# Diffusion backbone on one core: the last modulation vectors computed in the last recurrence head instead of in the first ConvGLU

## The chip, the cores and the metric

The kernel runs on one core of a Trainium2 chip. The metric is the device time of one execution in microseconds. The planner (the framework's scheduler) orders the instructions of every engine when the kernel is built, from their program order, their priorities and a timeline that it works out itself; the order of an engine's instructions is then fixed, and semaphores let each wait for its operands. A change of the program can therefore move instructions far from the lines it touches.

## What is computed

Two layers over 512 latent tokens and 256 context tokens of width 1024. Layer 0 mixes tokens by windowed attention, layer 1 by a gated linear recurrence in both directions with 8 heads; each layer ends with a ConvGLU. Every sub-layer is a norm, scaled and shifted by vectors made from the conditioning. Cut to what matters here:

```python
for layer in range(DEPTH):
    last = layer == DEPTH - 1
    mod = jax.nn.silu(c) @ ada_w[layer] + ada_b[layer]
    mod_c = jax.nn.silu(c_ctx) @ ada_w[layer] + ada_b[layer]
    sh1, sc1, g1, sh2, sc2, g2 = jnp.split(mod[:, None, :], 6, axis=-1)
    ...
    hx = rms_norm(x, norm1_g[layer]) * (1.0 + sc1) + sh1
    ...
        yx, yc = hgrn2_bidir(hx, hc, hgrn_w_in[j], hgrn_w_out[j], hgrn_o_gain[j], lb_sched[layer], not last)
    x = x + g1 * yx
    hx2 = rms_norm(x, norm2_g[layer]) * (1.0 + sc2) + sh2
    x = x + g2 * conv_glu(hx2, ffn_w_up[layer], ffn_conv_w[layer], ffn_conv_b[layer], ffn_w_down[layer])
```

The six vectors of a layer are computed in three ranges of 2048 columns of `ada_w`: range 0 holds sh1 and sc1, range 1 g1 and sh2, range 2 sc2 and g2. Layer 1's sc2 is first used where the recurrence's output is scaled for the second ConvGLU, its g2 in that ConvGLU's down product.

## The kernel before

**Products.** Each large product is done in three passes: weights and activations are split into a high part (a ScalarE copy, `wh`, L117 or L140) and a low part (a VectorE subtraction, `wl`, L118 or L141), and PE multiplies high by high, high by low, low by high (`mm_steps`, L170). A weight block comes by one or two DMAs on SP's queue into a raw buffer of 8 KB per partition (`load_raw`, L95, tile `wr`, two buffers in all), and is split into operand tiles of 512 columns, taken in turn from the pools in the list `self.wsp` (`operand`). In the recurrence that list holds three pools in turn: `ws0` with four buffers, `wsC` and `wsD` with two each. The splits are given a priority 180 instructions ahead of their place (`W_AHEAD`).

**Vectors.** `ada_steps` (L307 to L324) computes one range: eight loads of 1 MB of `ada_w` into the same two raw buffers (tile `wada`), after each of them four plain fp32 products of 32 output rows side by side in the array (`ada`, L309), then a VectorE copy to SBUF (`adas`, L314), four transposes (`adat`, L318), the addition of the bias (`mod`, L324) and, for range 2, the scale of the second norm (`gs`). It is a generator that yields after each step, so that another loop can lay its steps between its own. Ranges 0, 1 and 2 of layer 1 are drawn by the first ConvGLU: one step ahead of each of its 22 column tiles (`next(side)`), and one in each of its first five down rounds.

**The recurrence** (`hgrn`). For each head `front` makes the forget gates (`pf`) and the query (`pq`), `back` the value (`pv`, transposed as `pvT`, copied to `v`) and the gate (`pgate`), all from PE into PSUM tiles of two banks in the pool `pj`, two buffers. `scan` is the head's chain of dependent steps. It has seven levels: in each, ScalarE gathers the keys into `Y`, PE makes small products (`lv` at L1134 in levels 0 to 4, `at` at L1147 and L1149 in levels 5 and 6), and VectorE multiplies the queries (`Q`, L1158) and the keys (`K`, L1159) for the next level. Then the tail: transposes (`kT`), state products (`U`), the states (`S`, L1204 and L1206), the output (`po`), its norm (`osq`, `oss`, `or`, `oR`), and `oT`, which is split into `oh` (L1240, L1241). Its PSUM tiles are those of the pools `sc` and `lv`, one bank each, two buffers.

While a head's chain runs, the steps of the generator `fill` are traced between its own: `back` of this head and `front` of the next; for the last head, in place of the next `front`, `begin_out`. That starts the output product `ho`: its columns come in four pairs (`dp`), each in one tile of `pj`, and for pairs 0 and 1 the parts of heads 0 to 6 are done while the last head's chain still runs. When the last head's `oh` is there, `hgrn_out` adds its part to pairs 0 and 1 and does pairs 2 and 3; behind each pair VectorE adds to the stream (`xl`, L908), ScalarE scales it by `gs` (`y`, L375), and the operands of the second ConvGLU are made from that (`combos`, `hs`, L383, L384, L396).

**Pools of PSUM.** In the recurrence `pj` takes the first four of the eight banks, then `sc` two and `lv` two. Before and after it one pool takes all eight for a ConvGLU.

Of the kernel before, what the change touches and what calls it, by code (L numbers as in the profile page):

```python
# [8 lines left out]
F32 = mybir.dt.float32  # L9
# [5 lines left out]
PSUM = bass.MemoryType.PSUM  # L15

P = 128
D = 1024
KT = D // P
# [49 lines left out]
def f(t):  # L69
    return t.bitcast(F32)  # L70


class Kernel:
    def __init__(self, tc, a, dbg=None):
        self.tc, self.nc, self.a, self.dbg = tc, tc.nc, a, dbg or {}
# [958 lines left out]
    def hgrn(self, hn, R, acc, hb, pj, lv, sc):  # L1034
        nc, a = self.nc, self.a
        win = a["hgrn_w_in"][0]
        act = lambda k: (hn[:, 0, k], hn[:, 1, k])
        es = ExitStack()
        h1 = self.pool(es, "h1", 1)
# [6 lines left out]
        rows = self.row_factor(acc, False, h1, sc, "sc", 512, R, 1.0, (h1, "dg"))  # L1046
# [18 lines left out]
        def front(h, s):  # L1065

            wf = self.load_w([cw(1024 + h * P), cw(2048 + h * P)])
            wq, s["wv"] = self.load_w([cw(h * P), cw(3072 + h * P)])
            T = h1.tile([P, 2, TOK], F32, tag="T", name="T")
            K2 = h1.tile([P, 2, TOK], F32, tag="K2", name="K2")  # L1070
            for dr in range(2):
                ps = pj.tile([P, 1024], F32, tag="pj", name="pf")
                yield from steps(ps, wf[dr], NFULL)
                for _ in rows:
                    pass
                z = h1.tile([P, TW], F32, tag="sg", name="z", bufs=2)
                nc.vector.tensor_tensor(z, ps[:, 0:TW], R, op=ALU.mult)
                i = 1 - dr
                nc.scalar.activation(T[:, i, 0:LAT], z[:, 0:LAT], AF.Sigmoid, bias=z[:, SH:SH + 1])
                nc.scalar.activation(T[:, i, LAT:TOK], z[:, C0:TW], AF.Sigmoid, bias=z[:, SH + 1:SH + 2])  # L1080
                nc.gpsimd.tensor_scalar(T[:, i], T[:, i], self.lb[:, 1, h:h + 1], self.lb[:, 0, h:h + 1], op0=ALU.mult, op1=ALU.add)
                nc.gpsimd.tensor_scalar(K2[:, i], T[:, i], -1.0, 1.0, op0=ALU.mult, op1=ALU.add)
            yield from half(s, wq, "q")
            Q2 = h2.tile([P, 2, LAT], F32, tag="Q2", name="Q2")
            nc.vector.tensor_tensor(Q2, ap(s["q"][:, 0:1], 0, (0, 2), (1, LAT)), T[:, :, 0:LAT], op=ALU.mult)
            KK = h1.tile([P, LAT], F32, tag="KK", name="KK")
            nc.vector.tensor_tensor(KK, K2[:, 0, 0:LAT], K2[:, 1, 0:LAT], op=ALU.add)
            s.update(T=T, K2=K2, Q2=Q2, KK=KK)

        def back(h, s):  # L1090

            wg, = self.load_w([cw(4096 + h * P)])
            ps = pj.tile([P, 1024], F32, tag="pj", name="pv")
            yield from steps(ps, s["wv"], NFULL)
            z = h1.tile([P, TW], F32, tag="sg", name="zv", bufs=2)
            nc.vector.tensor_tensor(z, ps[:, 0:TW], R, op=ALU.mult)
            for lo, hi, c in ((0, LAT, SH), (C0, TW, SH + 1)):
                nc.scalar.activation(z[:, lo:hi], z[:, lo:hi], AF.Identity, bias=z[:, c:c + 1])
            yield from half(s, wg, "gate")
            pt = pj.tile([P, 1024], F32, tag="pj", name="pvT")  # L1100
            for i in range(6):
                t0 = i * P if i < NQ else C0 + (i - NQ) * P
                nc.tensor.transpose(pt[:, i * P:(i + 1) * P], z[:, t0:t0 + P], self.ident)
            v = h2.tile([P, 6, P], F32, tag="v", name="v")
            nc.scalar.activation(v, pt[:, :TOK].rearrange("p (t c) -> p t c", c=P), AF.Copy)
            s["v"] = v
# [128 lines left out]
        wout = a["hgrn_w_out"][0]  # L1235
        part = [None, [], []]

        def split_o(h):
            oh = part[0]
            nc.scalar.activation(oh[:, 0, h], oT[:, h], AF.Copy)  # L1240
            nc.vector.tensor_tensor(oh[:, 1, h], oT[:, h], f(oh[:, 0, h]), op=ALU.subtract)  # L1241

        def begin_out():

            part[0] = oh = hb.tile([P, 2, KT, LAT], F32R, tag="hn", name="oh1")
            for dp in range(2):
                w = self.load_w([self.wcols(wout, d * P, P) for d in (dp, dp + 4)])
                ps = pj.tile([P, 1024], F32, tag="pj", name="ho")
                part[1].append(w)
                part[2].append(ps)  # L1250
                for j in range(2):
                    out = [(ps[:, 512 * j:512 * j + 512], 0)]
                    for k in range(KT - 1):
                        if dp == 0 and j == 0:
                            split_o(k)
                        yield from self.mm_steps(w[j], (k,), lambda k: (oh[:, 0, k], oh[:, 1, k]), out, k == 0, False)

        ss = [{} for _ in range(KT + 1)]
        for _ in front(0, ss[0]):
            pass  # L1260
        for h in range(KT):
            def fill(h=h):
                yield from back(h, ss[h])
                yield from (front(h + 1, ss[h + 1]) if h + 1 < KT else begin_out())

            rest = fill()
            for n in scan(h, ss[h]):
                for _ in range(n):
                    next(rest, None)
            for _ in rest:  # L1270
                pass
# [36 lines left out]
    def run(self, stop=99):  # L1308
        nc, a = self.nc, self.a
        top = ExitStack()  # L1310
# [12 lines left out]

        xp = self.pool(top, "xp")
        self.xl = xp.tile([P, KT, LAT], F32, tag="xl", name="xl")
        self.wsp.append(self.pool(top, "wsC", 2))
        Rp = self.pool(top, "Rp", 1)
        pjs = ExitStack()
        pj = self.pool(pjs, "pj", 2, PSUM)
        hB = ExitStack()  # L1330
        hb = self.pool(hB, "hB")
        h1 = hb.tile([P, 4, 2, 4, 386], F32R, tag="hn", name="hs0")
# [3 lines left out]
        es = ExitStack()  # L1336
        tmp = self.pool(es, "tmpA", 1)
        acp = self.pool(es, "accA", 1)
        acc = Rp.tile([P, TOK], F32, tag="acc", name="acc0")
        hs = [*(h1[:, i] for i in range(4)), h2]  # L1340
# [8 lines left out]
        bk = self.pool(pjs, "bkA", 8, PSUM)  # L1349
        h3 = self.pool(rs, "hs2", right=True).tile([P, 2, 2, 4, 386], F32R, tag="hs", name="hs5")  # L1350
        hs += [h3[:, i] for i in range(2)]
        gp = self.pool(es, "gpA", 5)
        R = Rp.tile([P, 772], F32, tag="R", name="R0")
        rows = self.row_factor(acc, False, tmp, bk, "ps", 512, R, -1.0, (gp, "g"))
# [11 lines left out]
            self.scaled(1, 0, d, hn2[0], False)  # L1366

        self.ap_, self.ap_tag = Rp, "acc"
        self.ffn(0, hs, R, rows, False, tmp, acp, bk, gp, done0, (x for r in (0, 1, 2) for x in self.ada_steps(1, r, bk, "ps", 512)))
        if stop == 3:  # L1370
            self.dump_x(); rs.close(); es.close(); hss.close(); hB.close(); pjs.close(); top.close(); return
        R = Rp.tile([P, TW], F32, tag="R", name="R1")
# [1 line left out]
        es.close()  # L1374
        hss.close()
        pjs.close()
        pj = self.pool(pjs, "pj", 2, PSUM)
        es = ExitStack()
        self.wsp.append(self.pool(top, "wsD", 2, right=True))
        e2 = ExitStack()  # L1380
        sc = self.pool(e2, "sc", 2, PSUM)
        lv = self.pool(e2, "lv", 2, PSUM)
        part = self.hgrn(hn2[0], R, accs[0], hb, pj, lv, sc)
        hc = self.pool(rs, "hC", 1, right=True)
        hs1 = hc.tile([P, 7, 2, 4, 258], F32R, tag="hs", name="hs3")
        hs = [hs1[:, i] for i in range(7)]
# [6 lines left out]
        R = Rp.tile([P, 516], F32, tag="R", name="R2")  # L1393
# [4 lines left out]
        es = ExitStack()  # L1398
        tmp = self.pool(es, "tmpB", 2)
        acp = self.pool(es, "accB", 1)  # L1400
        gp = self.pool(es, "gpB", 9)
        self.wsp.append(self.pool(es, "wsE", 2))
        self.wd = self.pool(es, "wd", 2)
        bk = self.pool(es, "bkB", 8, PSUM)
        rows = self.row_factor(acc, True, tmp, bk, "ps", 512, R, -1.0, (gp, "g"))
# [17 lines left out]
    def dump_x(self):  # L1423
        if "dbg" in self.dbg:
            self.nc.sync.dma_start(out=self.dbg["dbg"][:, :, :LAT], in_=self.xl)
            self.nc.sync.dma_start(out=self.dbg["dbg"][:, :, LAT:], in_=self.xc)


class _Multi:
# [5 lines left out]
    def tile(self, shape, dt, tag=None, name=None, **kw):  # L1435
        return (self.p1 if tag in self.tags else self.p0).tile(shape, dt, tag=tag, name=name, **kw)
# [23 lines left out]
```

## Time and profile before

| | |
|---|---|
| time, median of 3 runs | 1842.15 us (1841.32 to 1843.34) |
| time of the profiled execution | 1841.45 us |
| its span, first to last instruction | 1838.9 us |
| mean granted TensorE clock | 0.989 |
| loads: `ada_w`, ranges of 2048 columns | 40 of 1 MB |
| loads: `hgrn_w_out` | 8 of 512 KB |
| HBM read over the span | 162.27 MB |

The span's stages, by their first instructions: attention to 360 us, its output product to about 460, the first ConvGLU to 989, the recurrence to 1435, its output product to 1462, the second ConvGLU to the end.

In the lines of the profile, PE is TensorE's matmuls, PEld its weight loads, DVE is VectorE, ACT ScalarE, POOL GpSimd, SPq SyncE's DMA queue. A row of the timeline has the start, the duration, the engine, the line of the kernel, the operation, output and inputs by name, partitions x elements and count, and in brackets the idle time before it and what ended that. Busy time is the union of an engine's instructions. Two views differ in what they count: a window gives the busy time of every engine in a stretch, the chain of waits only what nothing else covered.

### The profile page before, as it was taken

The page shows a single profiled execution, that of the slowest core. Times are in us where ns is not written, and L with a number is a line of the kernel's source. Part 1 is how long each engine was busy: PE and PEld are TensorE (multiplying, and loading weights), DVE is VectorE, ACT ScalarE, POOL GpSimd, SP SyncE. Part 2 cuts the span into 40 slices and gives each one's busy share as a digit, 9 for nine tenths or more (in the row PEclk, how much of TensorE's full clock was granted, in tenths as well). Part 3 has the DMA queues.
Part 4 walks back from the last instruction along what each step waited for, and adds up shares of the span by engine and source line. Part 5 has one row for each costly group of instructions (what it writes and reads, how often), then busy time and mean ns, then how long its engine had stood idle before and what let it go on. Part 6 is the DMA issues. An engine that isn't in the chain of part 4 may idle for free.

```text
span 1838.9 us, 32347 instructions
## 1 busy us (share of the span) xinstructions
PE 1770.4 (96%) x13062; PEld 1547.0 (84%) x13062; DVE 1325.5 (72%) x2420; ACT 839.3 (46%) x1754; POOL 239.8 (13%) x233
## 2 busy tenths in 40 slices
PE   6999999998999999999999999999999889999998
PEld 4986786687889888888898888989887688999997
DVE  6576676467668676757677667777676789999985
ACT  4345555465534343424445333333233555555553
POOL 1233333101100010100000101111110011011100
PEclk9999999999999999999999999999999889999999
DMA  9204104332343343333314111122121132423322
GB/s 313 69 24 155 53 24 152 89 104 72 115 124 104 114 133 97 102 105 127 115 44 121 55 39 43 51 58 59 47 58 47 46 115 86 118 84 102 94 81 81
DMA packets 204611, 166.44 MB, mean 91 GB/s; under 512 B 5341, under 2 KB 198446, under 8 KB 199342
## 3 DMA queue, kind: packets, MB, share of 16 engines
q1 hardware_dynamic: 196800, 160.47, 28.5%
q10 hardware_dynamic: 7662, 3.92, 0.7%
q8 instruction: 102, 1.67, 0.4%
q14 instruction: 47, 0.39, 0.1%
HBM read 162.27 MB, written 2.10 MB: 89 GB/s over the span
## 4 chain that ended last, share of the span: by engine, by line
PE 87%; DVE 5%; DMA 4%; ACT 2%; issue 1%; POOL 0%; SPq 0%; ACTq 0%; DVEq 0%; POOLq 0%
PE dn L170 16%; PE pZ L188 15%; PE pf L170 8%; PE pV L188 7%; PE pjq L611 4%; PE pv L170 4%; PE pY L188 4%; PE ao L170 3%; PE ho L170 3%; PE pq L170 3%; PE pv L837 3%; PE pt L829 2%; PE ada L309 2%; PE pgate L170 2%; PE kv L611 2%; DMA wr<-in_ffn_w_up 2%
## 5 line engine op out<-in xcount | busy, mean ns | idle before, releaser
L188 PE MATMUL pZ<-hs,wh 128*128 128x386 f32 (+1 forms) x1408 | 317.7, 316 | 9.4 <-ACT wh L140 4.2
L140 ACT ACTIVATE wh<-wr 128x512 fp32r<-128x512 f32 x264 | 164.3, 629 | 223.8 <-PE pZ L188 54.3
L170 PE MATMUL dn<-g,wh 128*128 128x512 f32 (+1 forms) x1056 | 266.2, 358 | 0.2 <-ACT wh L117 0.2
L188 PEld LDWEIGHTS pZ<-hs,wh 128*128 128x128 f32 x1408 | 241.9, 192 | 27.4 <-issue 10.9
L117 ACT ACTIVATE wh<-wr 128x512 fp32r<-128x512 f32 (+2 forms) x192 | 113.5, 602 | 281.3 <-DMA wr<-in_hgrn_w_in 61.8
L188 PE MATMUL pZ<-hs,wl 128*128 128x386 f32 (+1 forms) x704 | 218.1, 313 | 3.7 <-DVE wl L141 3.6
L141 DVE TENSOR_TENSOR wl<-wr,wh 128x512 fp32r<-128x512 f32 x264 | 188.9, 722 | 45.1 <-ACT wh L140 44.7
L170 PEld LDWEIGHTS dn<-g,wh 128*128 128x128 f32 x1056 | 173.3, 189 | 26.5 <-ACT wh L117 0.5
L923 POOL TENSOR_TENSOR gg<-gg,R 128x772 f32<-128x772 f32 (+1 forms) x44 | 83.2, 1890 | 760.1 <-DVE gg L922 747.2
L118 DVE TENSOR_TENSOR wl<-wr,wh 128x512 fp32r<-128x512 f32 (+2 forms) x192 | 128.3, 680 | 63.9 <-ACT wh L117 63.6
L188 PE MATMUL pV<-hs,wh 128*128 128x386 f32 (+1 forms) x704 | 161.1, 315 | 6.0 <-DVE hs L384 2.7
L170 PE MATMUL dn<-g,wl 128*128 128x512 f32 (+1 forms) x528 | 158.8, 356 | 0.0
L188 PEld LDWEIGHTS pZ<-hs,wl 128*128 128x128 f32 x704 | 133.3, 190 | 7.8 <-DVE wl L141 5.8
L188 PEld LDWEIGHTS pV<-hs,wh 128*128 128x128 f32 x704 | 120.8, 191 | 10.0 <-DVE hs L384 3.7
L170 PE MATMUL pf<-hn,wh 128*128 128x512 f32 (+1 forms) x512 | 117.6, 345 | 2.9 <-DVE xc L1024 1.9
L188 PE MATMUL pV<-hs,wl 128*128 128x386 f32 (+1 forms) x352 | 110.5, 314 | 1.4 <-DVE wl L141 1.4
L170 PEld LDWEIGHTS dn<-g,wl 128*128 128x128 f32 x528 | 87.5, 188 | 13.6
L1024 DVE SCALAR_TENSOR_TENSOR xl<-dn,mod,xl 128x512 f32<-128x512 f32 x96 | 71.3, 745 | 32.5 <-PE dn L170 32.3
L170 PEld LDWEIGHTS pf<-hn,wh 128*128 128x128 f32 x512 | 79.4, 189 | 15.5 <-DVE xc L1024 2.2
L188 PE MATMUL pY<-hs,wh 128*128 128x386 f32 (+1 forms) x352 | 81.6, 318 | 2.8 <-ACT wh L140 2.8
L611 PE MATMUL pjq<-wh,hn 128*128 128x256 f32 x384 | 77.8, 291 | 0.0
L188 PEld LDWEIGHTS pV<-hs,wl 128*128 128x128 f32 x352 | 67.1, 191 | 2.0 <-DVE wl L141 1.9
(298 smaller groups left out, 3851.1 us busy)
## 6 DMA issues: line engine op xcount, KB each, us to landing
wr<-in_ffn_w_up SPq DMA_DIRECT2D x88, 512.0 KB, 5.1
wada<-in_ada_w SPq DMA_DIRECT2D x40, 1024.0 KB, 4.8
wr<-in_hgrn_w_in SPq DMA_DIRECT2D x40, 512.0 KB, 4.0
wd<-in_ffn_w_down SPq DMA_DIRECT2D x20, 512.0 KB, 5.1
ar<-in_ada_w SPq DMA_DIRECT2D x32, 256.0 KB, 7.1
wr<-in_attn_w_in SPq DMA_DIRECT2D x6, 1024.0 KB, 7.8
wr<-in_ffn_w_down SPq DMA_DIRECT2D x12, 384.0 KB, 3.1
wr<-in_attn_w_out SPq DMA_DIRECT2D x8, 512.0 KB, 6.0
```

Source lines behind the costliest of these rows:

```text
L117: nc.scalar.activation(wh, src, AF.Copy)
L118: nc.vector.tensor_tensor(wl, src, f(wh), op=ALU.subtract)
L140: nc.scalar.activation(ops[i][0], src, AF.Copy)
L141: nc.vector.tensor_tensor(ops[i][1], src, f(ops[i][0]), op=ALU.subtract)
L170: nc.tensor.matmul(o, lhsT=wt, rhs=at[:, t0:t0 + o.shape[1]], start=(first and n == 0 and i == 0), stop=(last and n == len(ks) - 1 and i = ...
L188: self.nc.tensor.matmul(ps, lhsT=wt, rhs=at, start=(first and k == 0 and i == 0), stop=(k == nk - 1 and i == 2), skip_group_check=not first)
L309: nc.tensor.matmul(ps[32 * j:32 * j + 32, 0:512], lhsT=self.cs[:, k, :], rhs=raw[:, j * 512:(j + 1) * 512], start=(k == 0), stop=(k == KT ...
L611: nc.tensor.matmul(out, lhsT=x, rhs=y[:, wk], start=(start and k == 0 and j == 0), stop=(stop and k == KT - 1 and j == 2))
L829: nc.tensor.transpose(pt[:, j * P:(j + 1) * P], pr[j][:, b * P:(b + 1) * P], self.ident)
L837: nc.tensor.matmul(pv[a * HD:(a + 1) * HD, 0:256], lhsT=V[:, tl, g, :], rhs=pT[:, a * 256:(a + 1) * 256], start=(b == 0), stop=(b == len(t ...
L923: times = lambda eng, o, x, y: eng.tensor_tensor(o, x, y, op=ALU.mult)
L1024: nc.vector.scalar_tensor_tensor(x[:, d], o, self.modc(l, v, 5, d), x[:, d], op0=ALU.mult, op1=ALU.add)
```

## The change

Range 2 of layer 1 is taken out of the generator that the first ConvGLU draws from, and put into `begin_out`: there its steps are drawn one by one ahead of the products of pair 0 (`next(vectors, None)`), and the rest, if any, ahead of pair 1. Its two PSUM tiles become the two halves of one tile of `pj` (`_Halves`), its SBUF copy takes the tag `KK` of the recurrence's pool. The weights of both pairs are loaded at the beginning of `begin_out`, ahead of the vectors' loads. The steps of the last head's chain are traced under a priority 400 instructions ahead of their place; the other heads' are not. `sc` is opened ahead of `pj`, so that it has banks 0 and 1 and `pj` banks 2 to 5. `self.wsp` becomes a list in which `ws0`, with its four buffers, comes twice a turn.

```diff
         def begin_out():
             part[0] = oh = hb.tile([P, 2, KT, LAT], F32R, tag="hn", name="oh1")
+            self.ap_, self.ap_tag = h1, "KK"
+            vectors = self.ada_steps(1, 2, _Halves(pj.tile([P, 1024], F32, tag="pj", name="ada2")), "pj", 512)
+            part[1] = [self.load_w([self.wcols(wout, d * P, P) for d in (dp, dp + 4)]) for dp in range(2)]
             for dp in range(2):
-                w = self.load_w([self.wcols(wout, d * P, P) for d in (dp, dp + 4)])
+                w = part[1][dp]
+                for _ in vectors if dp else ():
+                    pass
                 ps = pj.tile([P, 1024], F32, tag="pj", name="ho")
-                part[1].append(w)
                 part[2].append(ps)
                 for j in range(2):
                     out = [(ps[:, 512 * j:512 * j + 512], 0)]
                     for k in range(KT - 1):
                         if dp == 0 and j == 0:
                             split_o(k)
+                        next(vectors, None)
                         yield from self.mm_steps(w[j], (k,), lambda k: (oh[:, 0, k], oh[:, 1, k]), out, k == 0, False)
...
             rest = fill()
-            for n in scan(h, ss[h]):
+            chain = scan(h, ss[h])
+            while True:
+                with self.tc.high_priority(offset=400) if h + 1 == KT else ExitStack():
+                    n = next(chain, None)
+                if n is None:
+                    break
                 for _ in range(n):
                     next(rest, None)
...
-        self.wsp.append(self.pool(top, "wsC", 2))
+        wsC = self.pool(top, "wsC", 2)
+        self.wsp.append(wsC)
...
-        self.ffn(0, hs, R, rows, False, tmp, acp, bk, gp, done0, (x for r in (0, 1, 2) for x in self.ada_steps(1, r, bk, "ps", 512)))
+        self.ffn(0, hs, R, rows, False, tmp, acp, bk, gp, done0, (x for r in (0, 1) for x in self.ada_steps(1, r, bk, "ps", 512)))
...
-        pj = self.pool(pjs, "pj", 2, PSUM)
         es = ExitStack()
-        self.wsp.append(self.pool(top, "wsD", 2, right=True))
+        wsD = self.pool(top, "wsD", 2, right=True)
+        self.wsp = [self.ws0, wsC, self.ws0, wsD]
         e2 = ExitStack()
         sc = self.pool(e2, "sc", 2, PSUM)
+        pj = self.pool(e2, "pj", 2, PSUM)
         lv = self.pool(e2, "lv", 2, PSUM)
...
-        self.wsp.append(self.pool(es, "wsE", 2))
+        self.wsp = [self.ws0, wsC, self.ws0, wsD, self.pool(es, "wsE", 2)]
...
+class _Halves:
+    def __init__(self, t):
+        self.parts = [t[:, 0:512], t[:, 512:1024]]
+    def tile(self, *a, **kw):
+        return self.parts.pop(0)
```

## The prediction

> **What bounds the kernel now.** I read the page first, then the stages by windows, then the last head of the recurrence in order of time.
>
> ```profile
> span 1838.9 us, 32347 instructions
> PE 1770.4 (96%) x13062; PEld 1547.0 (84%) x13062; DVE 1325.5 (72%) x2420; ACT 839.3 (46%) x1754; POOL 239.8 (13%) x233
> PE 87%; DVE 5%; DMA 4%; ACT 2%; issue 1%; POOL 0%; SPq 0%; ACTq 0%; DVEq 0%; POOLq 0%
> ```
>
> PE is busy for 1770.4 of 1838.9 us, and 87% of the chain that ended last is PE. So a step pays if it takes work off a stretch in which PE is full and puts it into one in which PE stands still; 1838.9 - 1770.4 = 68.5 us of standing is all there is to fill. The windows tell where (window, length, busy us and instructions of PE, PEld, DVE, ACT, POOL, then granted clock, DMA share, GB/s):
>
> ```profile
> 460.00:989.00 529.00, 519.64 (x2957) 469.56 (x2956) 378.14 (x622) 231.70 (x444) 45.97 (x21) 1.00 0.35 109
> 989.00:1378.00 389.00, 388.01 (x3853) 346.45 (x3854) 271.82 (x460) 132.08 (x274) 45.89 (x39) 1.00 0.19 54
> 1378.00:1462.00 84.00, 75.19 (x564) 59.56 (x563) 57.03 (x113) 36.56 (x84) 2.69 (x10) 0.94 0.18 51
> 1462.00:1540.00 78.00, 65.09 (x446) 61.21 (x447) 67.84 (x122) 42.50 (x90) 7.04 (x5) 0.87 0.30 88
> ```
>
> The first ConvGLU (460 to 989) is PE's: 98% busy, DVE 71%. Heads 0 to 6 (989 to 1378) have 1 us of idle. The last head and the output product (1378 to 1462) have 84.00 - 75.19 = 8.81 us, the first tiles of the second ConvGLU (1462 to 1540) 12.91 us, and in both the granted clock is below 1.
>
> ```profile
> 1378.00:1396.00 18.00, 15.43 (x229) 13.74 (x229) 12.23 (x21) 10.20 (x22) 1.38 (x1) 1.00 0.22 60
> 1396.00:1417.70 21.70, 21.70 (x165) 16.75 (x166) 13.16 (x22) 3.83 (x7) 0.00 (x0) 1.00 0.18 49
> 1417.70:1435.50 17.80, 12.09 (x69) 9.19 (x69) 7.59 (x21) 2.95 (x8) 1.31 (x9) 0.80 0.00 1
> ```
>
> The tail once more, in stretches of 5 us:
>
> ```profile
> 1425.00:1430.00 5.00, 2.10 (x18) 1.85 (x16) 1.60 (x3) 0.60 (x1) 1.01 (x1) 0.85 0.00 0
> 1430.00:1435.00 5.00, 3.56 (x6) 1.65 (x7) 1.38 (x2) 0.93 (x3) 0.31 (x8) 0.50 0.00 0
> 1435.00:1440.00 5.00, 5.00 (x15) 3.35 (x14) 4.03 (x7) 4.08 (x10) 0.00 (x0) 0.62 0.20 57
> ```
>
> 2.57 us of the idle lie before 1396 and 5.71 us after 1417.7, where the last head's chain runs alone; between them PE is full. Behind the idle the clock falls to 0.50: busy time times the clock that is missing, 2.10 x 0.15 + 3.56 x 0.50 + 5.00 x 0.38, is 4.0 us more. So the tail of the last head costs some 10 us, and by the rows below it comes late because its steps stand behind the output product on PE.
>
> ```profile
> 1403.34 0.68 DVE L1158 TENSOR_TENSOR Q<-Q,T 128x512 f32<-128x512 f32 x1
> 1409.08 0.69 DVE L1158 TENSOR_TENSOR Q<-Q,T 128x512 f32<-128x512 f32 x1 [2.10 <-PE at L1149]
> 1409.69 0.95 DVE L1159 TENSOR_TENSOR K<-K,T 128x768 f32<-128x768 f32 x1
> 1415.19 0.27 PE L1147 MATMUL at<-Q,K 128*64 128x64 f32 x1
> 1433.38 1.65 PE L170 MATMUL ho<-oh,wh 128*128 128x512 f32 x3 [1.44 <-ACT oh L1240]
> ```
>
> Level 5 needs Q and K of level 4, ready at 1403.34 + 0.68 = 1404.0; its products end just before the Q at 1409.08, some 4.6 us later. Level 6 needs those of level 5, ready at 1409.69 + 0.95 = 1410.6, and starts at 1415.19, again 4.6 us late. Between stand only matmuls of ho. The chain's end lets the last part of ho start, at 1433.38.
>
> **The change part by part.**
>
> *Vectors out of the first ConvGLU.* Range 2 takes eight groups of eight matmul records (four products of two passes) and four transposes; the first and the last group of the eight, and the transposes:
>
> ```profile
> 756.54 1.07 PE L309 MATMUL ada<-wada,cs 128*32 128x512 f32 x8
> ...
> 912.80 1.07 PE L309 MATMUL ada<-wada,cs 128*32 128x512 f32 x8
> ...
> 920.27 0.60 PE L318 MATMUL adat<-cst,adas 128*128 128x128 f32 x4
> ```
>
> 8 x 1.07 + 0.60 = 9.2 us of PE in a stage that PE bounds: **-9.2**. The DVE copy, the two additions and the two scale steps go too, and eight loads of 1 MB from SP's queue; PE waits for neither there, so nothing for those.
>
> *The same work in the last head.* **+9.2** of PE; its loads are weighed with the rivals. Three things hang on it. The tile takes one of the two pj buffers, so the second pair of the output product must wait until either the vectors or the first pair are through; a matmul of it that PE's queue holds too early keeps the chain's products behind it waiting. The DVE copy of the vectors waits for the eighth group, and the splits of later weights stand behind it. And the wout loads of pairs 2 and 3 and the first loads of the second ConvGLU now stand behind eight loads in SP's queue.
>
> *The chain first.* At an offset of 400 the chain goes ahead of ho and of the weight splits (180). The two lags of 4.6 us go; I count on about 10 us of earlier end. That costs PE nothing, since ho is only moved behind: its second pair, 42 matmuls, now lies where PE stood still. Of the 8.81 us of idle I keep 3 (the chain has pieces of its own without cover, and a load may be late), and of the 4.0 us of clock 0.5: **-9.3**. The bounds are 0 (the work fills only what was full) and -12.8 (all of it).
>
> [...]
>
> *The start of the second ConvGLU.* Nothing is changed in its work, but its wait is for DVE, as the DVE share of 1462 to 1540 shows (67.84 of 78.00), and DVE has 10.2 us of idle between 1417.7 and 1435.5. If the first pair of ho is finished 10 us earlier, its additions, scaled halves and combinations move into that idle.
>
> ```profile
> 1470.00:1475.00 5.00, 1.21 (x4) 0.62 (x3) 5.00 (x12) 2.69 (x6) 1.01 (x1) 0.50 0.00 0
> 1475.00:1480.00 5.00, 4.90 (x16) 3.63 (x17) 4.33 (x8) 2.58 (x5) 0.00 (x0) 0.53 0.72 230
> ```
>
> 3.79 us of idle and 1.21 x 0.50 + 4.90 x 0.47 = 2.9 us of clock hang on that: 6.7. Bounds 0 and the stage's whole idle, -12.9; I take **-4**, nearer to the row, since DVE stays full for a part of it.
>
> *The pools.* With sc below pj, the banks of the first tiles differ at both ends of the recurrence.
>
> ```profile
> PE pZ L188 <- DVE xl L908: 1.6, 1, 1.6
> PE pf L170 <- DVE xc L1024: 1.9, 1, 1.9
> ```
>
> The wait of pZ for the last xl addition is a wait for a bank of pj that the second ConvGLU takes over; sc's banks, free long before, would come first: -1.6. The wait of pf can go, stay or grow by as much, for I don't know which bank ends last: -1.9 to +1.9. I take 0 for both together, as the first may only uncover the next wait. *The operand buffers* rotate eight deep in the recurrence in place of six (three pools in turn, the two small ones with two each), and ten deep in the second ConvGLU in place of eight. PE has 1 us of idle in heads 0 to 6, so nothing there; for the second ConvGLU between 0 and a few us, within the bounds above.
>
> Sum: -9.2 + 9.2 - 9.3 - 4 = -13.3, so 1841.45 (the profiled execution; span 1838.9 and 2.5 around it) becomes 1828.2. The median of the three runs shown is 0.7 above the profiled execution: **1829**.
>
> **The rivals.** *The vectors come late* (slower). ACT's first scaled half needs the second norm's scale, which these vectors make:
>
> ```profile
> 1436.45 0.71 ACT L375 ACTIVATE y<-xl,gs 128x512 f32<-128x512 f32 x1
> ...
> DMA to landing us min/median/max: 4.7/4.8/5.0
> ...
> 158.12 1.92 PE L309 MATMUL ada<-wada,cs 128*32 128x512 f32 x16
> 183.75 1.07 PE L309 MATMUL ada<-wada,cs 128*32 128x512 f32 x8
> ...
> 1380.74 6.50 DMA wr<-in_hgrn_w_out
> 1395.90 6.77 PE ho L170 x28
> ...
> 1380.33 0.99 SPq L95 DMA_DIRECT2D wr<-in_hgrn_w_out  x2
> 1401.80 0.99 SPq L95 DMA_DIRECT2D wr<-in_hgrn_w_out  x2
> 1437.72 0.99 SPq L95 DMA_DIRECT2D wr<-in_ffn_w_up  x2
> ```
>
> The first chunk can follow the first pair's weights (1380.33), the second the second pair's (1401.80 at the latest), landing 4.8 us on, at 1406.6. In attention the eight groups took 183.75 - 158.12 = 25.6 us with two buffers, 3.7 each. At that pace the other six end near 1430, before 1436.45: no loss there. Pair 2's weights are issued behind the seventh group, near 1426, and land 6.50 us on, near 1433. PE has work from 1396 until 1436 without them: 96 matmuls of ho at 6.77 / 28 us (23.2), 9.2 of vectors, some 8 of the chain (the 12.09 busy us of 1417.7 to 1435.5 less ho's first matmuls). With one buffer at a time a chunk takes 4.8 + 1.07 = 5.9 and they end at 1443, 7 us late, which eats most of the gain. It turns slower when they end over 9.2 us late, that is over 6.2 us a chunk; at 8 us they end at 1456, all DVE work of the output stage shifts by 19, and 1841 - 9 + 19, less what DVE takes back, gives about 1848. For it speaks that one bank pair and two raw buffers carry everything; against it, the 3.7.
>
> [...]
>
> *The vectors only push ho out* (no change). Their 9.2 us run between 1396 and 1417.7, where PE is full, the second pair of ho finds no bank until the chain is over, and the tail stays open: -9.2 + 9.2 = 0, 1842. For it speaks the one buffer that two tiles share; against it, that the first pair frees another.
>
> *The offset does nothing* (faster, less). The chain ends as before because the steps of the level, not PE's order, are long; ho still fills 5 of the idle's 8.8 us: about 1837. The two lags of 4.6 us speak against it.
>
> *DVE's relief is whole* (faster, more): the second ConvGLU's first stall goes with its clock and the bank waits too: -21, 1821.
>
> **How the numbers follow.** Within 0.2% (3.7 us, about what a measurement of this kernel can tell from no change) is 1838.5 to 1845.8. Forecast, 1823 to 1836: 0.55. Whole relief: 0.11. Offset does nothing: 0.11. Only pushed out: 0.13. Late vectors: 0.10. Faster 0.77, same 0.13, slower 0.10. The range reaches from the whole relief, with 2 us for a new order elsewhere, to half of the way between no change and the late vectors: 1819 to 1844.
>
> **What would show it.** In the first ConvGLU, PE busy lower by 9 us and nothing else. In the last head, levels 5 and 6 starting within 1 us of their Q and K, the chain's end before 1424 on the old axis less 9, eight groups of ada between about 1396 and 1430, no window of clock 0.5 ahead of the output stage. Wrong would be: ada groups 6 us apart, PE waiting for wout or for a pj bank, or the scaled halves starting after the chain's end because of gs.

## The result, and the profile after

The changed kernel takes 1824.72 us (median of 4 runs, 1823.13 to 1826.87), the kernel before on the same chip 1842.59 us (4 runs, 1841.32 to 1843.34). The ratio is 0.9901 (95% interval 0.9886 to 0.9916): 17.9 us faster, where 13.3 were forecast on the profiled execution. The profiled execution took 1823.13 us. Head of its page, the span and the busy time of each engine:

```profile
span 1821.1 us, 32329 instructions
PE 1762.3 (97%) x13062; PEld 1542.3 (85%) x13062; DVE 1327.0 (73%) x2420; ACT 840.9 (46%) x1754; POOL 253.2 (14%) x233
```

PE's busy time fell by 1770.4 - 1762.3 = 8.1 us and its idle time from 68.5 to 58.8, 9.7 us. The work is the same (13062 matmul records in both), so the same matmuls took 8.1 us less; the granted clock of the windows below shows where.

Where that lies is read from the stages in windows, cut at about the same events in both kernels: the first ConvGLU, then (heads 0 to 6 left out) the last head with the output product, and the start of the second ConvGLU (window, length, busy us and instructions of PE, PEld, DVE, ACT, POOL, granted clock, DMA share, GB/s). Before:

```profile
448.50:988.90 540.40, 531.04 (x3023) 480.74 (x3019) 385.79 (x633) 236.03 (x453) 48.23 (x22) 1.00 0.35 109
...
1378.00:1461.50 83.50, 75.19 (x564) 59.56 (x563) 56.54 (x112) 36.54 (x84) 2.69 (x10) 0.94 0.18 51
1461.50:1539.00 77.50, 64.09 (x438) 60.21 (x439) 67.33 (x121) 42.36 (x90) 7.04 (x5) 0.87 0.31 89
```

After:

```profile
448.50:978.90 530.40, 520.98 (x2961) 478.12 (x2960) 389.46 (x629) 237.71 (x458) 48.91 (x22) 1.00 0.31 95
...
1367.30:1452.80 85.50, 79.42 (x633) 59.27 (x631) 57.31 (x116) 36.45 (x85) 2.32 (x10) 1.00 0.44 136
1452.80:1522.00 69.20, 62.53 (x444) 58.70 (x444) 64.14 (x117) 41.42 (x89) 13.93 (x5) 0.93 0.36 99
```

The first ConvGLU is 10.0 us shorter, all of it PE's busy time (531.04 to 520.98). The last head with the output product is 2.0 us **longer**, although its clock is 1.00 and its idle fell from 8.31 to 6.08. The start of the second ConvGLU is 8.3 us shorter, by idle (13.41 to 6.67) and clock (0.87 to 0.93). So two gains of nearly the same size, and only one of them comes from the moved vectors as such.

For all kernels of this study I use the same cuts, from the first and last starts of the matmuls `pf`, `pq`, `ho` and `dn`. All in us:

| kernel | first ConvGLU (from 448.5 to first pf) | heads 0 to 6 (first pf to last pq) | last head and output (last pq to last ho) | start of second ConvGLU (last ho to first dn) | rest (to last dn) |
|---|---|---|---|---|---|
| before | 540.4 | 378.8 | 93.4 | 67.8 | 303.6 |
| after | 530.4 | 378.2 | 95.3 | 59.7 | 302.6 |

The last head is followed as steps in order of time in the changed kernel (start, duration, engine, line, operation, count, idle time before it and what ended that):

```profile
1383.44 1.06 PE L309 MATMUL ada<-wada,cs 128*32 128x512 f32 x8 [1.46 <-ACT oh L1240]
1389.29 0.68 DVE L1158 TENSOR_TENSOR Q<-Q,T 128x512 f32<-128x512 f32 x1
1394.55 0.22 PE L1147 MATMUL at<-Q,K 128*32 128x32 f32 x1
1395.08 0.69 DVE L1158 TENSOR_TENSOR Q<-Q,T 128x512 f32<-128x512 f32 x1 [3.89 <-PE at L1149]
1399.34 0.69 DVE L1158 TENSOR_TENSOR Q<-Q,T 128x512 f32<-128x512 f32 x1 [2.69 <-PE at L1149]
1406.95 0.39 PE L1215 MATMUL po<-Q,S 128*128 128x128 f32 x2
1408.79 1.06 PE L309 MATMUL ada<-wada,cs 128*32 128x512 f32 x8 [1.45 <-DMA wada<-in_ada_w]
1409.79 0.49 PE L1216 MATMUL po<-Q,S 128*128 128x128 f32 x2
1412.53 0.63 ACT L117 ACTIVATE wh<-wr 128x512 fp32r<-128x512 f32 x1 [1.15 <-DMA wr<-in_hgrn_w_out]
1413.07 0.58 ACT L1221 ACTIVATE osq<-po 128x512 f32<-128x512 f32 x1
1414.64 0.23 DVE L333 SCALAR_TENSOR_TENSOR gs<-mod,par 128x8 f32<-128x8 f32 x2
1416.14 0.69 DVE L556 TENSOR_TENSOR dg<-cst,or 128x512 f32<-128x512 f32 x1 [1.18 <-POOL or L441]
1421.46 1.02 PE L559 MATMUL oR<-dg,cst 128*128 128x512 f32 x2
1424.48 0.68 DVE L1241 TENSOR_TENSOR oh<-oT,oh 128x512 fp32r<-128x512 f32 x1
1426.46 1.41 DVE L908 SCALAR_TENSOR_TENSOR xl<-ho,mod,xl 128x512 f32<-128x512 f32 x2 [1.30 <-PE ho L170]
1427.29 0.71 ACT L375 ACTIVATE y<-xl,gs 128x512 f32<-128x512 f32 x1
```

The steps `oh` and `xl` of the kernel before, in the same view:

```profile
1433.36 0.69 DVE L1241 TENSOR_TENSOR oh<-oT,oh 128x512 fp32r<-128x512 f32 x1 [0.70 <-ACT oh L1240]
1435.49 1.60 DVE L908 SCALAR_TENSOR_TENSOR xl<-ho,mod,xl 128x512 f32<-128x512 f32 x2 [1.44 <-PE ho L170]
```

Read it from the top. The Q of level 4 is ready at 1389.29 + 0.68 = 1389.97, but the products of level 5 begin at 1394.55: the lag of 4.6 us is still there, now filled with matmuls of `ho` and of `ada`. The priority changes the order of PE's list, but the list is still fixed when the kernel is built. Later `po` stands cut in two behind the eighth group, which waits 1.45 us for its load (1408.79); `osq` stands on ACT behind a weight split that waits 1.15 us for `wout` (1412.53); and `oR` starts at 1421.46, 4.6 us after its `dg` is ready (1416.14 + 0.69), behind matmuls of `ho`. Measured from the last `pq` (1357.1, before 1367.7), the chain ends with `oh` at 1424.48 + 0.68 - 1357.1 = 68.1, before, at 1433.36 + 0.69 - 1367.7 = 66.4. It does not end earlier. Level 6 does start earlier, 1398.60 - 1357.1 = 41.5 us behind the last `pq` against 1415.19 - 1367.7 = 47.5 before, but from there to the end of `oh` the chain takes 26.6 us in place of 18.9.

### The profile page after: what moved, and what is told of

The parts are those of the page before. It is cut to its first block, busy times and chain, and to the rows that moved or that the text cites. A ratio compares the mean times of both kernels' runs of the same rounds, so it can differ in the third digit from the quotient of the medians.

```text
span 1821.1 us, 32329 instructions
## 1 busy us (share of the span) xinstructions
PE 1762.3 (97%) x13062; PEld 1542.3 (85%) x13062; DVE 1327.0 (73%) x2420; ACT 840.9 (46%) x1754; POOL 253.2 (14%) x233
## 4 chain that ended last, share of the span: by engine, by line
PE 87%; DVE 5%; DMA 4%; ACT 2%; issue 1%; SPq 0%; POOL 0%; ACTq 0%; DVEq 0%; POOLq 0%
PE dn L170 16%; PE pZ L188 15%; PE pf L170 8%; PE pV L188 7%; PE pjq L611 4%; PE pv L170 4%; PE pY L188 4%; PE ao L170 4%; PE pgate L170 3%; PE pq L170 3%; PE pv L837 3%; PE pt L829 2%; PE ho L170 2%; PE kv L611 2%; PE ada L309 2%; DMA wr<-in_ffn_w_up 2%
## 5 line engine op out<-in xcount | busy, mean ns | idle before, releaser
L923 POOL TENSOR_TENSOR gg<-gg,R 128x772 f32<-128x772 f32 (+1 forms) x44 | 92.5, 2101 | 727.1 <-DVE gg L922 637.9
L118 DVE TENSOR_TENSOR wl<-wr,wh 128x512 fp32r<-128x512 f32 (+2 forms) x192 | 132.2, 698 | 70.3 <-ACT wh L117 58.2
L188 PEld LDWEIGHTS pY<-hs,wh 128*128 128x128 f32 x352 | 59.3, 189 | 10.5 <-ACT wh L140 8.7
```

The source lines that it names most:

```text
L118: nc.vector.tensor_tensor(wl, src, f(wh), op=ALU.subtract)
L188: self.nc.tensor.matmul(ps, lhsT=wt, rhs=at, start=(first and k == 0 and i == 0), stop=(k == nk - 1 and i == 2), skip_group_check=not first)
L923: times = lambda eng, o, x, y: eng.tensor_tensor(o, x, y, op=ALU.mult)
```

## The experiments

Two explanations for the second gain stood against each other at first: that of the prediction (the chain's priority lets VectorE's work of the output move forward), and a rival, that the operand list with `ws0` twice a turn does it by itself. For the last head the question was what the priority and the vectors are worth alone and together. For the second of these, two theories: L, that groups of `ada` waiting for their loads hold up PE's list when the priority is missing; and P', that without the priority PE's list lays `ho`'s second pair and the vectors ahead of the chain's steps, loads or not.

The experiments ran on other chips than the first comparison; there the kernel before takes 1845 to 1847 us and its first ConvGLU 2 to 5 us more, so ratios to the kernel before on the same chip are compared. An interval stands beside each. The results in one table, with the stages of each profiled execution, columns as above:

| kernel | time us, runs | before us | ratio (95%) | first ConvGLU | last head and output | start of second | rest |
|---|---|---|---|---|---|---|---|
| b_vec | 1840.43, 7 | 1847.17 | 0.9961 (0.9948 to 0.9975) | 535.8 | 98.4 | 67.9 | 303.6 |
| b_rot | 1837.68, 4 | 1847.17 | 0.9950 (0.9933 to 0.9967) | 542.8 | 95.1 | 61.4 | 301.4 |
| b_prio | 1844.32, 10 | 1847.17 | 0.9986 (0.9977 to 0.9995) | 544.9 | 90.6 | 67.8 | 303.8 |
| a_noprio | 1837.05, 4 | 1847.17 | 0.9948 (0.9933 to 0.9963) | 532.4 | 107.6 | 59.8 | 302.5 |
| a_norot | 1839.45, 10 | 1846.31 | 0.9965 (0.9956 to 0.9975) | 532.2 | 96.3 | 68.5 | 305.3 |
| a_norotE | 1839.46, 10 | 1846.31 | 0.9965 (0.9954 to 0.9975) | 531.2 | 103.0 | 69.3 | 306.1 |
| a_nopool | 1829.36, 4 | 1846.31 | 0.9910 (0.9885 to 0.9934) | 532.6 | 101.3 | 59.0 | 302.6 |
| a_again | 1830.00, 5 | 1844.97 | 0.9917 (0.9903 to 0.9932) | 533.8 | 95.7 | 59.7 | 302.5 |
| b_rotprio | 1834.39, 5 | 1844.97 | 0.9943 (0.9931 to 0.9956) | 545.1 | 91.0 | 62.1 | 301.2 |
| a_rot0 | 1820.65, 4 | 1844.97 | 0.9870 (0.9855 to 0.9885) | 523.7 | 99.8 | 59.2 | 304.2 |
| np_1load | 1834.27, 4 | 1844.97 | 0.9946 (0.9932 to 0.9959) | 532.7 | 105.2 | 59.4 | 302.5 |

A stage is read from one execution alone: a_nopool has 101.3 in the last head where a_again has 95.7, though the two give each engine its instructions in the same order and differ in time by less than their intervals. Differences of 5 us in that column alone prove nothing; the other columns agree within 3.4 us among kernels on one chip that don't differ there.

### One part at a time on the kernel before

**b_vec**: only the vectors move, with their halves of a `pj` tile and the early weights, as in the diff of the change.

```diff
+            vectors = self.ada_steps(1, 2, _Halves(pj.tile([P, 1024], F32, tag="pj", name="ada2")), "pj", 512)
+            part[1] = [self.load_w([self.wcols(wout, d * P, P) for d in (dp, dp + 4)]) for dp in range(2)]
             for dp in range(2):
-                w = self.load_w([self.wcols(wout, d * P, P) for d in (dp, dp + 4)])
+                w = part[1][dp]
...
-        self.ffn(0, hs, R, rows, False, tmp, acp, bk, gp, done0, (x for r in (0, 1, 2) for x in self.ada_steps(1, r, bk, "ps", 512)))
+        self.ffn(0, hs, R, rows, False, tmp, acp, bk, gp, done0, (x for r in (0, 1) for x in self.ada_steps(1, r, bk, "ps", 512)))
```

> The kernel before with the vectors moved and nothing else. Theory A (the work leaves a full stage and fills the idle of the last head by itself): the first ConvGLU 10 us shorter, as in the changed kernel, the last head and output stage no more than 3 us longer, the start of the second ConvGLU as before: 1842 - 10 + 3 = 1835 us or less. Theory B (the vectors need the deeper operand turn, since the second chunk waits for the second pair's weights to be split): the last head and output stage 6 to 10 us longer, 1838 to 1842 us.

Measured 0.9961: 7 us. The first ConvGLU gives its part, the last head takes about half of it back (98.4 against 93.4, in these two executions), and the start of the second ConvGLU is untouched (67.9 against 67.8). The gain is the one of theory A, and the 5 us of the last head lie between the two theories: neither holds as it was written.

**b_rot**: only the two operand lists.

```diff
-        self.wsp.append(self.pool(top, "wsD", 2, right=True))
+        wsD = self.pool(top, "wsD", 2, right=True)
+        self.wsp = [self.ws0, wsC, self.ws0, wsD]
...
-        self.wsp.append(self.pool(es, "wsE", 2))
+        self.wsp = [self.ws0, wsC, self.ws0, wsD, self.pool(es, "wsE", 2)]
```

> The kernel before with the two new operand lists and nothing else. Theory R (the 8 us that the start of the second ConvGLU lost come from the deeper turn of operand buffers): the stretch from the end of ho to the first dn is 5 to 8 us shorter, 1834 to 1837 us. Theory D (they come from VectorE work that starts earlier because of the chain): no more than 2 us shorter, 1840 to 1842 us. Either way heads 0 to 6 change by under 1 us.

Measured 0.9950: 9 us, the largest of the three parts. It lies at the start of the second ConvGLU (61.4 against 67.8) and in the rest (301.4 against 303.6), with no help from the chain.

**b_prio**: only the priority.

```diff
-            for n in scan(h, ss[h]):
+            chain = scan(h, ss[h])
+            while True:
+                with self.tc.high_priority(offset=400) if h + 1 == KT else ExitStack():
+                    n = next(chain, None)
```

> The kernel before with the last head's chain at priority 400 and nothing else. Theory P (the prediction's: the chain then ends some 10 us earlier and ho fills its tail): 8 to 13 us less, 1829 to 1834 us. Theory N (the planner's own timeline sets the order, and what it has wrong isn't mended by a priority): within 3 us of before, 1839 to 1845 us.

Measured 0.9986: 2.6 us, as theory N has it. The last head shrinks by 2.8 (90.6 against 93.4), and the chain ends 63.6 us behind the last `pq` in place of 66.4: 2.8 us earlier, not 10. Its end still runs alone:

```profile
1434.07 1.10 PE L559 MATMUL oR<-dg,cst 128*128 128x512 f32 x2 [2.22 <-DVE dg L556]
1436.60 1.65 PE L170 MATMUL ho<-oh,wh 128*128 128x512 f32 x3 [1.44 <-ACT oh L1240]
```

PE stands for 2.22 and 1.44 us before these two, as the kernel before did: in its list no `ho` stands between `kT` and the end of the chain, for the parts of heads 0 to 6 are used up by then. The priority by itself finds no more work to put there.

**a_noprio**: the changed kernel with `with ExitStack():` in place of the priority.

> The changed kernel with the priority of the last head's chain taken back and nothing else. Theory P: 5 us or more above the changed kernel's 1824.7, so 1830 us or more. Theory N: within 3 us of it, 1822 to 1828 us.

Measured 0.9948 against 0.9901 and 0.9917 for the changed kernel: beside the vectors the priority is worth 6 to 9 us, not 2.6. Without it the last head takes 107.6. From its trace, in order of time:

```profile
1412.93 1.94 PE L309 MATMUL ada<-wada,cs 128*32 128x512 f32 x8 [2.46 <-DMA wada<-in_ada_w]
1414.80 4.57 PE L1199 MATMUL U<-v,kbt 128*128 128x128 f32 x20
1420.62 0.39 PE L1215 MATMUL po<-Q,S 128*128 128x128 f32 x2
1427.06 0.38 PE L1216 MATMUL po<-Q,S 128*128 128x128 f32 x2
1434.42 0.95 PE L1227 MATMUL oss<-cst,osq 128*128 128x2 f32 x8
```

Two causes are in these rows. A group of `ada` waits 2.46 us for its load in front of `U`, and the clock drops to 0.50 (`U` takes 4.57 us at a clock of 0.52, in the changed kernel 2.50 at 1.00). And `po` is interrupted from 1420.62 to 1427.06, `oss` stands until 1434.42, by matmuls of `ho`'s second pair. np_1load below takes the first of them away.

### The operand list

**a_norot** puts both lists back to those of before, **a_norotE** only that of the second ConvGLU:

```diff
-        self.wsp = [self.ws0, wsC, self.ws0, wsD, self.pool(es, "wsE", 2)]
+        self.wsp = [self.ws0, wsC, wsD, self.pool(es, "wsE", 2)]
```

> The changed kernel with both operand lists as before the change (three pools in turn in the recurrence, four in the second ConvGLU) and nothing else. Theory R (the deeper turn makes the 8 us at the start of the second ConvGLU): 6 to 10 us above the changed kernel's 1824.7, 1831 to 1835 us. Theory D (VectorE's earlier start makes them): within 2 us, 1823 to 1827 us.

> The changed kernel with four pools in turn, eight deep, in the second ConvGLU in place of ten deep; the recurrence keeps the new list. If the gain of theory R comes from the second ConvGLU's own list: as without both lists, 1831 to 1835 us. If it comes from the recurrence's list (weights of the output product split earlier, so that the second ConvGLU's loads can start earlier): within 2 us of the changed kernel, 1823 to 1827 us.

Both measured 0.9965: the one line costs the changed kernel more than half of its gain (0.9917 for a_again), and the recurrence's list adds nothing to that. The first 68.5 us behind the last `ho` in the kernel before, in a_norotE, in b_rot and in a_again (same columns as the windows above):

```profile
1461.50:1530.00 68.50, 55.09 (x375) 51.82 (x376) 58.37 (x105) 36.78 (x78) 5.67 (x4) 0.85 0.32 93
```

```profile
1461.10:1529.60 68.50, 53.55 (x369) 50.34 (x369) 56.35 (x104) 36.84 (x77) 6.29 (x4) 0.86 0.32 93
```

```profile
1466.30:1534.80 68.50, 61.89 (x440) 58.41 (x440) 63.75 (x116) 40.47 (x86) 7.63 (x5) 0.93 0.35 96
```

```profile
1456.40:1524.90 68.50, 61.75 (x441) 57.95 (x441) 63.47 (x117) 41.56 (x89) 13.92 (x5) 0.93 0.36 100
```

With the short list PE does 375 and 369 matmul records in that stretch, with the long one 440 and 441, whether vectors and priority are there (a_norotE, a_again) or not (before, b_rot). (The profiled execution of a_norotE is the longest of its ten, so its other stages are not read.) What PE waits for in the same stage in the kernel before (total us, times, longest):

```profile
PE pZ L188 <- ACT wh L140: 3.5, 2, 3.0
PE pV L188 <- ACT hs L383: 2.7, 1, 2.7
PE pZ L188 <- ACT gg L930: 2.4, 1, 2.4
```

and in the changed kernel:

```profile
PE nss L536 <- DVE acc L527: 2.3, 1, 2.3
PE pZ L188 <- DVE xl L908: 1.5, 1, 1.5
PE pZ L188 <- ACT t L943: 1.2, 1, 1.2
```

The wait for a weight split (`wh`) is gone, and those for ScalarE's `hs` and `gg`. In a_norotE the wait of `pZ` for `wh` is there again (3.6 us), in b_rot 2.0 us of such waits are left. The longest one before, 3.0 us, ends with a split that ScalarE made at 1500.60, directly behind an activation of the ConvGLU (L988) for which it had waited 1.13 us: this split was not ahead at all. The runs show that the one line makes the gain; why a deeper list does is argued from the program: in a list of pools used in turn, a place whose pool has two buffers and stands once in the list can be ahead by two turns only; `ws0` has four buffers but stood once, so two of them were never needed. With `ws0` twice the turn has five places with two buffers each, ten instead of eight splits ahead.

**a_nopool** opens `pj` ahead of `sc` again.

```diff
+        pj = self.pool(pjs, "pj", 2, PSUM)
         es = ExitStack()
...
         sc = self.pool(e2, "sc", 2, PSUM)
-        pj = self.pool(e2, "pj", 2, PSUM)
```

> The changed kernel with pj below sc again, as before the change. The order of all engines' instructions is then the same, only banks and waits differ. If the turn of the pools takes a wait away: 1 to 3 us above 1824.7. If not: within 1 us; the two waits of PE, pf for xc and pZ for xl, are in the changed kernel as before it, which speaks for this one.

Measured 0.9910 against 0.9901 and 0.9917: no difference that can be seen, though an interval of 4.5 us to either side cannot rule out the 1 to 3 us of the first theory. The wait of `pZ` for the last `xl` is in the changed kernel too (1.5 us, quoted above).

**a_again** is the changed kernel once more, on the chip of the last four.

> The changed kernel once more, on the same chip as the next three, to read them against. Its ratio to before was 0.9901 on another chip; every theory expects 0.989 to 0.992 here.

Measured 0.9917 (0.9903 to 0.9932), beside 0.9901 (0.9886 to 0.9916) on the first chip: the two intervals overlap.

### What the vectors are worth, and why the priority matters beside them

**b_rotprio**: lists and priority on the kernel before (the diffs of b_rot and b_prio together), the vectors stay in the first ConvGLU.

> The changed kernel with the vectors left in the first ConvGLU (the kernel before with both operand lists and the chain's priority). It gives what moving the vectors is worth beside the other parts. If their 9 to 10 us of the first ConvGLU come nearly for free in the last head, as in the prediction: 7 to 10 us above the changed kernel. If most of it is given back there, as the stages of the runs so far have it (last head and output stage 95.3 us with everything, 90.6 with the priority alone): 4 to 6 us above it.

Measured 0.9943 against 0.9917 for the whole change on the same chip: 4.4 us (1834.39 - 1830.00) is what the move of the vectors adds to the other two, with intervals that just touch. The stages of the two profiled executions say how: 545.1 - 533.8 = 11.3 us less in the first ConvGLU, 95.7 - 91.0 = 4.7 us more in the last head. The second difference is no larger than what two executions of one order showed; but as 11.3 us left the first ConvGLU and the time fell by 4.4, a good part came back.

**np_1load**: a_noprio, with range 2 computed from its first chunk alone, so that seven of its eight loads go while all its matmuls stay.

```diff
         for k in range(KT):
-            raw = self.wp.tile([P, 2048], F32, tag="wr", name="wada")
-            nc.sync.dma_start(out=raw, in_=self.a["ada_w"][l, k * P:(k + 1) * P, r * 2048:(r + 1) * 2048])
+            if k == 0 or (l, r) != (1, 2):
+                raw = self.wp.tile([P, 2048], F32, tag="wr", name="wada")
+                nc.sync.dma_start(out=raw, in_=self.a["ada_w"][l, k * P:(k + 1) * P, r * 2048:(r + 1) * 2048])
```

> The changed kernel without the chain's priority, and with the vectors computed from their first chunk alone: one load of ada_w in range 2 in place of eight, all matmuls kept. Without the priority the last head and output stage took 107.6 us, with it 95.3. Theory L (groups of the vectors that wait for their loads stand in PE's queue ahead of the chain's last products; the priority only moves the chain past them): with the loads gone the stage falls to 94 to 99 us though the priority is missing, and the time to that of the changed kernel or 3 us around it. Theory P' (the chain's own steps are served late without the priority, loads or not): the stage stays over 103 us.

Measured 0.9946 against 0.9948 for a_noprio, which ran on another chip: taking the loads away brings nothing that can be seen. From its trace (the line numbers are one higher):

```profile
1414.63 1.32 PE L1185 MATMUL kT<-cst,K 128*128 128x128 f32 x10 [1.08 <-DVE K L1160]
1415.71 0.70 PE L170 MATMUL ho<-oh,wh 128*128 128x512 f32 x2
...
1419.99 0.39 PE L170 MATMUL ho<-oh,wh 128*128 128x512 f32 x1
1420.22 2.39 PE L1200 MATMUL U<-v,kbt 128*128 128x128 f32 x20
```

`U` starts 4.3 us behind the end of `kT` (1415.95), behind `ho`, although no load holds anything up: the matmuls that do not wait take the place of those that waited. So L falls and P' holds: the loss is there without the loads. With them gone the list comes out in another order, so how much of the loss in a_noprio itself is its 2.46 us of waiting stays open. What the priority does beside the vectors is to keep PE's list from putting `ho`'s second pair into the chain: in the changed kernel `kT`, `U` and `po` follow each other with groups of `ada` alone between them. In b_prio, without the vectors, that pair is through before `kT`, and there is less to keep away. Where the pair is used up in the middle of the chain, the chain's tail runs alone, as in the kernel before: in np_1load PE stands for 2.23 us ahead of `oR` and for 1.4 us ahead of the last part of `ho`, `oR` takes 2.05 us (in the changed kernel 1.02) and a matmul of `ho` behind it 0.63 us until 1443, from there on 0.40, and over the stage (1360.9 to 1466.4) PE is busy for 98.23 us at a clock of 0.94, where the changed kernel (1357.1 to 1452.8) does the same work in 89.62 at 1.00.

### A version that beats both

**a_rot0**: the idea of the list carried to the first ConvGLU, where `ws0` and `wsC` alternate and the splits can be four ahead.

```diff
         wsC = self.pool(top, "wsC", 2)
-        self.wsp.append(wsC)
+        self.wsp = [self.ws0, wsC, self.ws0]
```

> The changed kernel with the list of the first ConvGLU and of the first output product turned as in the second: ws0 with its four buffers twice, wsC once, six deep in place of four. If PE's waits for splits there (4.3 us for wh and wl in the first ConvGLU's stage of the trace of before) come from the short turn, as in the second ConvGLU: 3 to 7 us below the changed kernel. If they come from VectorE, ScalarE and the two raw buffers: within 2 us of it.

Measured 1820.65 us, 0.9870 of the kernel before and 9.3 us (0.5%) under the changed kernel on the same chip, more than the 3 to 7 expected. What PE waits for in the first ConvGLU of a_again; in a_rot0 none of the three is left:

```profile
PE pY L188 <- ACT wh L140: 4.2, 5, 2.2
PE pZ L188 <- DVE wl L141: 3.0, 3, 1.5
PE pZ L188 <- ACT wh L140: 0.4, 1, 0.4
```

The stage in windows, of a_again and of a_rot0:

```profile
448.50:982.30 533.80, 524.17 (x2977) 480.96 (x2975) 390.97 (x633) 239.66 (x461) 48.90 (x22) 1.00 0.31 94
```

```profile
448.50:972.20 523.70, 522.36 (x2957) 479.68 (x2956) 392.01 (x630) 239.01 (x456) 46.34 (x22) 1.00 0.31 94
```

PE's idle goes from 9.63 to 1.34 us and the stage from 533.8 to 523.7. Some 4 us seem to come back in the last head (99.8 against 95.7), within what single executions of that stage differ by; PE stood there for 2.83 us before 1408.29.

## Why the prediction was right, and where not

**The first ConvGLU: -9.2 forecast, -10.0 measured.** Right, with its reason: PE's busy time fell by 10.06 us and its idle stayed (9.36 and 9.42). The 0.9 us over the eight groups and the transposes was not settled.

**The same work in the last head, and the chain first: +9.2 - 9.3 = -0.1 forecast, +1.9 measured.** The sum nearly held, the mechanism in part. As foreseen, the vectors fill idle time and the lost clock comes back: 1.00 in place of 0.94, no window at half clock ahead of the output stage. The 0.5 us of clock that the forecast kept was the author's estimate, and no run shows it: in the changed kernel's trace PE stands for 6.08 us between 1367.3 and 1452.8, in pieces of at most 1.46 us, at a clock of 1.00, while in a_noprio and a_nopool the clock was 0.50 behind stands of 1.95 to 2.46 us (last section). The step that failed is "the two lags of 4.6 us go; I count on about 10 us of earlier end", and with it the idle of which 3 us were to be kept. The lag before level 5 is still 4.6 us, that before level 6 is 2.0 (1396.64 to 1398.60), and the 6.0 us that the levels gained the tail lost, with 1.7 more, behind the eighth group's load, the `wout` split and `ho`. So the idle fell by 2.2 us (8.31 to 6.08) where 5.8 were counted. The clock gave more than was counted: about 9.2 us of matmuls came in and PE's busy time rose by 4.23 (75.19 to 79.42), which puts it, as an estimate, at 5.0 in place of 3.5. 9.2 - 5.0 - 2.2 is the 2.0 that was measured between the windows; that it lay near the forecast is in part luck. The test that the prediction set (levels within 1 us, the chain's end before 1424 less 9) came out against it: `oh` is ready at 1425.16, not before 1415. A larger offset does not put the chain first either: in a_rot0, 1000 or 4000 in place of 400 leaves the order of every engine as it is. So the moved vectors are not free in the last head: of the 11.3 us that leave the first ConvGLU between b_rotprio and a_again, 4.4 are left in the time.

**The start of the second ConvGLU: -4 forecast, -8.1 measured.** Here the mechanism was wrong and the term too small. The prediction had VectorE's additions of pair 0 move forward because the chain ends earlier. But the first addition lies 1461.5 - 1435.49 = 26.0 us ahead of the output product's end before, and 1452.8 - 1426.46 = 26.3 after: nothing moved. The gain is the operand list's: b_rot has it without the chain, a_norotE loses it with the chain's priority, a_noprio keeps it (59.8) with the chain late, and a_norot, whose chain ends 62.3 us behind its last `pq`, 4 us earlier than before, has 68.5. The prediction named that list as worth "between 0 and a few us, within the bounds above" and gave it no value of its own. That is the sentence that should have carried the term. The row that would have said so is the wait of `pZ` for `wh`, 3.5 us, the largest wait of the stage; it is not among the rows that the prediction rests on, which took the DVE share of 67.84 of 78.00 for the cause.

**The pools: 0 forecast, nothing seen.** a_nopool, within its interval. The wait of `pZ` for the last `xl`, which the prediction took for one that the turn of the pools would end, is 1.6 us before and 1.5 after.

**The recurrence's list: nothing forecast, nothing seen.** a_norot and a_norotE have the same ratio.

**Vectors late.** Did not occur. The groups run from 1383.44 to 1408.79, 25.35 / 7 = 3.6 us apart, as in attention (3.7), and `gs` is ready near 1414.9, ahead of the first scaled half at 1427.29. So the bound of 6.2 us a chunk was never near; the price of 8 us assumed there was not tested.

**The sum.** Against the forecast the stages differ by -0.8 (first ConvGLU), +2.0 (last head), -4.1 (start of the second ConvGLU) and -1.6 (heads 0 to 6 and the rest, at which nothing was forecast), together -4.5: 13.3 became 17.8 of span. The total lay near by luck: the operand list stood in for a chain that did not end earlier.

## What to carry to other kernels

Where pools with different numbers of buffers are used in turn, the pool with the fewest buffers for its share of the turn sets, by the argument above, how far ahead the work can run; give the larger one more places in the list, and look for that whenever PE waits for a split while a raw weight is at hand. A priority moves instructions in a list that is fixed when the kernel is built, so it does not make a chain run "first": read from the trace how many matmuls still stand between a step's operand and the step, and check each part of a change alone before a gain is credited to its most visible part. Work moved into idle time pays only for the part of it that really falls there: here 11.3 us left one stage, and the time fell by 4.4.

## What the runs showed that was not expected

Short stands of PE were followed by half of the clock. In a_noprio PE stood for 2.46 us before 1412.93, and then had a clock of 0.50 to 0.52 for some 6 us, as the windows of that stretch show:

```profile
1412.90:1414.80 1.90, 1.87 (x9) 0.20 (x9) 0.00 (x0) 0.00 (x0) 0.00 (x0) 0.50 0.30 125
1414.80:1419.30 4.50, 4.50 (x25) 4.34 (x22) 1.33 (x4) 0.34 (x1) 0.00 (x0) 0.52 0.69 198
```

In a_nopool stands of 1.95 and 2.40 us in the last head were followed by a clock of 0.50, over 3.41 and 3.40 us:

```profile
1407.77 1.07 PE L309 MATMUL ada<-wada,cs 128*32 128x512 f32 x8 [1.95 <-DMA wada<-in_ada_w]
1421.85 1.13 PE L1227 MATMUL oss<-cst,osq 128*128 128x2 f32 x8 [2.40 <-ACT osq L1221]
...
1409.03:1412.44 3.41, 3.41 (x18) 3.41 (x17) 0.00 (x0) 1.53 (x4) 0.00 (x0) 0.50 0.99 358
1422.70:1426.10 3.40, 3.40 (x10) 2.72 (x11) 1.17 (x5) 0.00 (x0) 1.01 (x1) 0.50 0.26 64
```

At the same two places PE stands for 1.63 and 1.13 us in a_again, for 1.45 and 0.98 in the changed kernel's first profile, and the clock stays at 1.00. The length of one stand alone does not decide it in these runs: in the kernel before, the clock is 0.50 from 1428.53 to 1435.50, and at 1428.53 the stand of 2.22 us ahead of `oR` (1429.89) had lasted for 0.86 us, behind stands of 1.15 us (before 1423.43) and 0.69 us (before 1426.62). What decides it stays open.

So one order of instructions gives different lengths: 95.3, 95.7 and 101.3 us for the last head in three executions with the same order (after, a_again, a_nopool). From a_again to a_nopool PE's idle in that stage goes from 6.42 to 9.00 us, with 1.4 more for loads of `ada_w` and 1.3 more for `osq`, which stands on ScalarE behind splits that wait for `wout`; and its busy time goes from 89.38 to 92.40 for the same 699 records, at a clock of 0.97. Why the loads came later in that execution is not shown.
